# Emitting the very last load of a 90-degree rotation ahead of an output, and giving that output the freed load buffer

## The chip, the cores and the metric

The kernel runs on one core of one Trainium2 chip. The metric is the device time of one execution in microseconds (us). "Time" below is that figure; "landing", "issue" and all other moments are read from a profile of one execution and count from the start of its span. In the profile of the kernel before, the last landing stands at 1264.37, the span is 1265.4 and the time of that execution 1267.31, so a time is about 2.9 us above the last landing. "Landing" needs a word: a transfer is shared out among up to 16 DMA engines, and each of them leaves a record when its share has arrived. The last of these records is the landing of the transfer.

## The reference

```python
def setup_inputs():
    return {"x": np.random.randn(8192, 8192).astype(np.float32), "k": 1}

def reference(x, k):
    return np.rot90(x, k)
```

An 8192 x 8192 matrix of 4-byte values is read once (268 MB) and written once (268 MB), turned by 90 degrees.

## The kernel before

The matrix is cut into macro tiles of 1024 x 4096. For each, eight loads of 128 rows (2 MB each) go out on SP's queue. VectorE reverses each row block by 128-column blocks into small "ar" tiles, PE (the matrix engine) transposes these into PSUM, ScalarE copies PSUM into an output tile "ot" and issues its store, also 2 MB. The last macro tile is cut into two of half height, here called A and B. Each has four loads (LA0 to LA3, LB0 to LB3) and four stores (A0 to A3, B0 to B3). M0 to M7 are the stores of the last full macro tile.

```python
a_pool = ctx.enter_context(tc.tile_pool(name="a_pool", bufs=2))   # load buffers
r_pool = ctx.enter_context(tc.tile_pool(name="r_pool", bufs=63))  # reversed chunks
o_pool = ctx.enter_context(tc.tile_pool(name="o_pool", bufs=3))   # output buffers
...
def load(r0, rt, c0):            # a generator: one row block for each next()
    ...
    for t in range(rt):
        ...
        a = a_pool.tile([P, W], dt, tag="a")     # (early loads: o_pool)
        nc.sync.dma_start(out=a[:], in_=x[...])
        for j in range(W // CH):
            ar = r_pool.tile([P, CH // P, P], dt, tag="ar")
            nc.vector.tensor_copy(out=ar[:], in_=...)   # the reversal
            chunks[t, j] = ar
        yield chunks

def store(r0, rt, c0, chunks, end):   # a generator: one output for each next()
    ...
    for i, g0 in enumerate(range(0, W // P, G)):
        if end and i % 2:
            ot = a_pool.tile([P, F], dt, tag="a")
        else:
            ot = o_pool.tile([P, F], dt, tag="o")
        ...                                  # 32 transposes, 2 copies
        nc.scalar.dma_start(out=dst, in_=...)
        yield
...
*_, chunks = load(*before_last)                    # LA0 .. LA3
outputs = store(*before_last, chunks, True)
rows = load(*last)
for _ in range(last[1] - 1):
    next(rows)                                     # LB0 .. LB2
next(outputs)                                      # A0
chunks = next(rows)                                # LB3
for _ in outputs:                                  # A1 .. A3
    pass
for _ in store(*last, chunks, True):               # B0 .. B3
    pass
```

There is one reversed chunk more (64) than there are tiles for them (63). So LB3's last reversal needs a chunk that A0's transposes give back, and A0 has to stand ahead of that reversal in the program.

Of the kernel before, what the change touches and what calls it, by code (L numbers as in the profile page):

```python
# [2 lines left out]

# [5 lines left out]

P = 128  # L10




R = 1024
RT = R // P
LAST = [4, 4]
W = 4096
CH = 512
F = 4096  # L20
FP = 2048


def whole_reads(nc):






    for fn in nc.m.functions:
        for block in fn.blocks:
            for n, ins in enumerate(block.instructions):
                if not isinstance(ins, mybir.InstDMACopy):
                    continue
                src = ins.ins[0]
                ap = [list(d) for d in src.ap]
                if len(ap) == 3 and ap[2][0] == 1 and ap[1][0] == ap[2][1]:
                    ap = [ap[0], [1, 1], [1, ap[1][1] * ap[2][1]]]
                    block.instructions[n] = copy.replace(  # L40
                        ins,
                        ins=[copy.replace(src, ap=ap)],
                        ant_dge_precooked=False,
                    )


def macro_tiles(N, M):

    tiles = [(r0, RT, c0) for r0 in range(0, N, R) for c0 in range(0, M, W)]
    r0, _, c0 = tiles.pop()  # L50
    for n in LAST:
        tiles.append((r0, n, c0))
        r0 += n * P
    return tiles


@with_exitstack
def kernel(
    ctx: ExitStack,
    tc: tile.TileContext,  # L60
    x: bass.AP,
    k: bass.AP,
    out: bass.AP,
):
    nc = tc.nc
    assert k == 1, f"only k=1 supported, got {k}"
    nc.at_finalize(whole_reads)

    N, M = x.shape
    dt = x.dtype  # L70

    consts = ctx.enter_context(tc.tile_pool(name="consts", bufs=1))
    ident = consts.tile([P, P], dt)
    make_identity(nc, ident)

    a_pool = ctx.enter_context(tc.tile_pool(name="a_pool", bufs=2))
    r_pool = ctx.enter_context(tc.tile_pool(name="r_pool", bufs=63))
    o_pool = ctx.enter_context(tc.tile_pool(name="o_pool", bufs=3))
    psum_pool = ctx.enter_context(
        tc.tile_pool(name="psum", bufs=2, space=bass.MemoryType.PSUM)  # L80
    )

    loads = 0

    def load(r0, rt, c0):





        nonlocal loads
        chunks = {}
        for t in range(rt):


            if loads < RT and loads % 5 >= 2:
                a = o_pool.tile([P, W], dt, tag="o")
            else:
                a = a_pool.tile([P, W], dt, tag="a")
            loads += 1  # L100
            nc.sync.dma_start(  # L101
                out=a[:], in_=x[r0 + t * P : r0 + (t + 1) * P, c0 : c0 + W]
            )
            for j in range(W // CH):
                ar = r_pool.tile([P, CH // P, P], dt, tag="ar")
                nc.vector.tensor_copy(  # L106
                    out=ar[:],
                    in_=a[:, j * CH : (j + 1) * CH].rearrange(
                        "r (b m) -> r b m", m=P
                    )[:, :, ::-1],  # L110
                )
                chunks[t, j] = ar
            yield chunks

    def store(r0, rt, c0, chunks, end):





        rows = rt * P
        PW = 1
        while 2 * PW * rows <= FP:
            PW *= 2
        G = PW
        while 2 * G * rows <= F:
            G *= 2
        for i, g0 in enumerate(range(0, W // P, G)):
            if end and i % 2:
                ot = a_pool.tile([P, F], dt, tag="a")  # L130
            else:
                ot = o_pool.tile([P, F], dt, tag="o")
            o = ot[:, : G * rows].rearrange("m (g f) -> m g f", g=G)



            lead = r0 == 0 and c0 == 0 and i in (4, 6)
            S = PW if lead or (end and r0 + rows == N and g0 + G == W // P) else G


            ps = {}

            def transposes(t, ws):
                for w in ws:
                    g = g0 + w
                    nc.tensor.transpose(  # L146
                        ps[w // PW][:, PW - 1 - w % PW, t * P : (t + 1) * P],
                        chunks[t, g * P // CH][:, g % (CH // P), :],
                        ident,
                    )  # L150

            def psum_tile(h):
                pt = psum_pool.tile([P, FP], mybir.dt.float32, tag="ps")
                ps[h] = pt[:, : PW * rows].rearrange("m (g f) -> m g f", g=PW)

            if i == 0 and (rt == RT or r0 + rows < N):
                for h in range(G // PW):
                    psum_tile(h)
                for t in range(rt):
                    transposes(t, range(G))  # L160
            for h in range(0, G, PW):
                if h // PW not in ps:
                    psum_tile(h // PW)
                    for w in range(h, h + PW):
                        for t in range(rt):
                            transposes(t, [w])
                nc.scalar.copy(o[:, G - PW - h : G - h, :], ps[h // PW])  # L167

                done = h + PW
                if done % S == 0:  # L170
                    top = M - c0 - (g0 + done) * P
                    dst = out[top : top + S * P, r0 : r0 + rows].rearrange(
                        "(g m) f -> m g f", g=S
                    )
                    nc.scalar.dma_start(  # L175
                        out=dst, in_=o[:, G - done : G - done + S, :]
                    )
            yield

    tiles = macro_tiles(N, M)  # L180
    *most, before_last, last = tiles
    for m in most:
        *_, chunks = load(*m)
        for _ in store(*m, chunks, False):
            pass


    *_, chunks = load(*before_last)
    outputs = store(*before_last, chunks, True)
    rows = load(*last)  # L190
    for _ in range(last[1] - 1):
        next(rows)
    next(outputs)
    chunks = next(rows)
    for _ in outputs:
        pass
    for _ in store(*last, chunks, True):
        pass


# [1 line left out]
_INS = ['x', 'k']  # L202
_OUTS = [((8192, 8192), 'float32')]

_NUMBERS = {'k': 1}


# [26 lines left out]
```

## Time and profile before

| | before |
|---|---|
| time, median of 6 runs | 1267.64 us (1267.44 to 1268.09) |
| bytes moved | 537 MB at 428 GB/s in mid-run |
| busiest compute engine | PE, 57% |
| A0's copies start / A0 issued | 1214.80 / 1218.46 us |
| last landing | 1264.37 us |

The prediction shows the page's lines on traffic and chain, the timeline of the tail and the DMA share by stretches. Two more lines of the page are needed to read them, those of the DMA issues: what is moved, who issues it, how often, the KB of one, and the median us from issue to landing.

```profile
a<-in_x_dram SPq DMA_DIRECT2D x128, 2048.0 KB, 16.6
out_dram<-ot ACTq DMA_DIRECT2D x125, 2048.0 KB, 25.7
```

A store takes 25.7 us from its issue until it has landed, although 2 MB at 428 GB/s are 4.9 us of traffic. By this sum most of a store's life is spent in a queue behind other transfers.

### The profile page before, as it was taken

Reading aid. Unit: us, or ns where it says so; the run is one execution under the profiler, and the core shown is the slowest. Engines: PE = TensorE matmul, PEld = TensorE weight load, DVE = VectorE, ACT = ScalarE, POOL = GpSimd, SP = SyncE. Lnnn points to the kernel's source line nnn. Section 1 sums busy time; section 2 is a strip of 40 time slices with the busy share of each in tenths; the row PEclk is TensorE's granted clock in tenths of the full one; section 3 lists DMA queues with packets and bytes.
Section 4 is the critical chain, followed back from the end, with each engine's and each line's share of the span. In section 5 each row is a group of like instructions: output and inputs, shape, how many; then the busy total and the mean of one; then the engine's idle time right before and its main releaser. Section 6 shows DMA issues by size and latency. Waiting matters only on the chain.

```text
span 1265.4 us, 10391 instructions
## 1 busy us (share of the span) xinstructions
PE 721.2 (57%) x4096; PEld 680.0 (54%) x4096; DVE 355.2 (28%) x1024; ACT 466.6 (37%) x257; POOL 0.7 (0%) x6
## 2 busy tenths in 40 slices
PE   1554555566555565565655666556555566566573
PEld 1453555566545565555645655456555555555573
DVE  4423223322232222322233222322233222332210
ACT  0432433433334333343334333343333433343354
POOL 0000000000000000000000000000000000000000
PEclk9977777767777768777687776866867867767787
DMA  9999999999999999999999999999999999999998
GB/s 398 428 428 430 427 428 429 429 431 428 428 429 427 430 429 430 428 430 429 428 428 430 429 430 428 428 430 428 429 430 428 429 427 430 426 428 427 428 380 355
DMA packets 37345, 537.55 MB, mean 425 GB/s; under 512 B 4144, under 2 KB 4144, under 8 KB 4144
## 3 DMA queue, kind: packets, MB, share of 16 engines
q10 hardware_dynamic: 18864, 268.44, 50.0%
q1 hardware_dynamic: 18432, 268.44, 49.7%
q8 instruction: 32, 0.52, 0.2%
q14 instruction: 17, 0.14, 0.0%
HBM read 268.44 MB, written 268.44 MB: 424 GB/s over the span
## 4 chain that ended last, share of the span: by engine, by line
DMA 84%; ACT 13%; issue 1%; PE 0%; ACTq 0%; DVE 0%; SPq 0%
DMA out_dram<-ot 81%; ACT ot L167 13%; DMA a<-in_x_dram 3%; PE pt L146 0%; ACTq L175 0%; DVE ar L106 0%; ACTq L167 0%; SPq L101 0%
## 5 line engine op out<-in xcount | busy, mean ns | idle before, releaser
L146 PE MATMUL pt<-ident,ar 128*128 128x128 f32 x4096 | 721.2, 357 | 526.2 <-ACT ot L167 470.2
L146 PEld LDWEIGHTS pt<-ident,ar 128*128 128x128 f32 x4096 | 680.0, 191 | 567.2 <-ACT ot L167 505.0
L167 ACT COPY ot<-pt 128x2048 f32<-128x2048 f32 x256 | 465.3, 1870 | 757.5 <-DMA out_dram<-ot 719.6
L106 DVE COPY ar<-a 128x512 f32<-128x512 f32 x1024 | 355.2, 420 | 861.8 <-DMA a<-in_x_dram 705.7
L167 ACT ACT_TABLE_LOAD x1 | 1.3, 1283 | 25.6 <-DVE ar L106 25.6
masks.py:199 POOL TENSOR_SCALAR_AFFINE_SELECT ident<-ident 128x128 f32<-128x128 f32 x1 | 0.3, 292 | 0.1
masks.py:197 POOL MEMSET ident<- 128x128 f32 x1 | 0.2, 204 | 0.3 <-POOLq L215 0.3
L215 POOL MEMSET const-bfloat16-1.0<- 128x1 bf16 x1 | 0.1, 101 | 0.0
L215 POOL MEMSET const-uint8-127<- 128x1 uint8 x1 | 0.1, 101 | 0.0
L215 POOL MEMSET const-float32-0.0<- 128x1 f32 x1 | 0.1, 98 | 0.2 <-issue 0.2
L215 POOL MEMSET const-float32-1.0<- 128x1 f32 x1 | 0.1, 98 | 0.0
## 6 DMA issues: line engine op xcount, KB each, us to landing
a<-in_x_dram SPq DMA_DIRECT2D x128, 2048.0 KB, 16.6
out_dram<-ot ACTq DMA_DIRECT2D x125, 2048.0 KB, 25.7
out_dram<-ot ACTq DMA_DIRECT2D x6, 1024.0 KB, 26.8
```

What stands on the lines that cost most here:

```text
L106: nc.vector.tensor_copy(out=ar[:], in_=a[:, j * CH : (j + 1) * CH].rearrange("r (b m) -> r b m", m=P)[:, :, ::-1],)
L146: nc.tensor.transpose(ps[w // PW][:, PW - 1 - w % PW, t * P : (t + 1) * P], chunks[t, g * P // CH][:, g % (CH // P), :], ident,)
L167: nc.scalar.copy(o[:, G - PW - h : G - h, :], ps[h // PW])
L215: nc = _bacc.Bacc("TRN2", target_bir_lowering=False, num_devices=1)
```

## The change

The last load, LB3, is emitted ahead of A0 and only its reversal stays behind. With LB3 placed, the next load buffer to come free is LB2's, and A0 takes it in place of an output buffer whose earlier store is still in flight. The intent is to let A0 be copied and stored earlier.

```diff
             nc.sync.dma_start(
                 out=a[:], in_=x[r0 + t * P : r0 + (t + 1) * P, c0 : c0 + W]
             )
+            yield chunks
             for j in range(W // CH):
...
         for i, g0 in enumerate(range(0, W // P, G)):
-            if end and i % 2:
+            if end and i % 2 == 0:
                 ot = a_pool.tile([P, F], dt, tag="a")
...
     rows = load(*last)
-    for _ in range(last[1] - 1):
+    for _ in range(2 * last[1] - 1):
         next(rows)
     next(outputs)
     chunks = next(rows)
```

## The prediction

> **What bounds the kernel now.** I name the outputs at the end: M0 to M7 are the eight 2 MB stores of the last full macro tile, A0 to A3 those of the last macro tile but one (half height), B0 to B3 those of the last. LB0 to LB3 are the four loads of the last tile. The change touches nothing before A0, so I read the page for the whole, then only the last 60 us.
>
> The page first: its head, the slices of moved bytes, the DMA queues and the chain.
>
> ```profile
> span 1265.4 us, 10391 instructions
> ...
> GB/s 398 428 428 430 427 428 429 429 431 428 428 429 427 430 429 430 428 430 429 428 428 430 429 430 428 428 430 428 429 430 428 429 427 430 426 428 427 428 380 355
> ...
> HBM read 268.44 MB, written 268.44 MB: 424 GB/s over the span
> ...
> DMA out_dram<-ot 81%; ACT ot L167 13%; DMA a<-in_x_dram 3%; PE pt L146 0%; ACTq L175 0%; DVE ar L106 0%; ACTq L167 0%; SPq L101 0%
> ```
>
> The kernel moves 537 MB at a flat 428 GB/s and no compute engine passes 57%: it is bound by the DMA engines. Only the last two of the 40 slices (31.6 us each) fall short, by 48 and 73 of 428 GB/s: 3.5 us and 5.4 us of full traffic. Anything that a change of the tail can win lies within those 9 us, 0.7% of the time.
>
> Next the timeline of the tail. Columns: start, length, engine, line, operation, and in brackets the idle time before and what ended it.
>
> ```profile
> 1205.64 3.63 ACT L167 COPY ot<-pt 128x2048 f32<-128x2048 f32 x2 [6.19 <-DMA out_dram<-ot]
> 1207.55 1.57 PEld L146 LDWEIGHTS pt<-ident,ar 128*128 128x128 f32 x8 [3.87 <-ACT ot L167]
> 1207.56 6.42 PE L146 MATMUL pt<-ident,ar 128*128 128x128 f32 x32 [3.63 <-ACT ot L167]
> 1209.30 0.55 ACTq L175 DMA_DIRECT2D out_dram<-ot  x1
> ...
> 1214.22 2.77 DVE L106 COPY ar<-a 128x512 f32<-128x512 f32 x8 [7.99 <-DMA a<-in_x_dram]
> 1214.80 3.63 ACT L167 COPY ot<-pt 128x2048 f32<-128x2048 f32 x2 [5.53 <-DMA out_dram<-ot]
> 1216.72 5.01 PEld L146 LDWEIGHTS pt<-ident,ar 128*128 128x128 f32 x32 [2.98 <-ACT ot L167]
> ...
> 1218.46 0.55 ACTq L175 DMA_DIRECT2D out_dram<-ot  x1
> ```
>
> The stores at 1209.30 and 1218.46 are M7 and A0. A0's copies stood from 1209.27 to 1214.80 for the landing of M5 (issued 1189.68, landed 1214.72), whose buffer they take: this is the wait that the change aims at. But A0's transposes, the 32 matmuls from 1207.56, ran until 1213.98 by the modelled ends.
>
> Then the DMA engines around it, in the view by stretches. The last two columns are their mean busy share and GB/s.
>
> ```profile
> 1215.00:1218.00 3.00, 1.28 (x6) 1.28 (x7) 2.00 (x6) 3.00 (x2) 0.00 (x0) 0.75 0.59 251
> 1218.00:1219.00 1.00, 1.00 (x7) 1.00 (x6) 0.00 (x0) 0.43 (x1) 0.00 (x0) 0.50 0.24 98
> 1219.00:1220.00 1.00, 1.00 (x7) 1.00 (x6) 0.00 (x0) 0.00 (x0) 0.00 (x0) 0.54 0.70 295
> 1220.00:1240.00 20.00, 17.46 (x151) 16.12 (x150) 0.00 (x0) 17.03 (x10) 0.00 (x0) 1.00 0.97 406
> 1240.00:1259.50 19.50, 6.91 (x61) 6.36 (x59) 0.00 (x0) 8.43 (x5) 0.00 (x0) 0.77 1.01 418
> 1259.50:1260.50 1.00, 0.00 (x0) 0.00 (x0) 0.00 (x0) 0.00 (x0) 0.00 (x0) 0.50 0.60 246
> 1260.50:1264.50 4.00, 0.00 (x0) 0.00 (x0) 0.00 (x0) 0.00 (x0) 0.00 (x0) 0.50 0.14 57
> ```
>
> There is a hole before A0's store: 3 x 0.41 + 0.76 + 0.30 = 2.3 us of idle mean. It looks like the prize. But a mean over 16 engines can hide which of them are idle, and the last row is the warning: for the final 4 us the share is 0.14, about 2 of 16. So I took the trace's landing records, of which each DMA leaves 16. First, 14th and last of the 16, in us:
>
> ```
> store   issued    first    14th     last     last minus last of the store before
> M5     1189.68  1199.7   1208.3   1214.72
> M6     1199.48  1209.4   1214.4   1219.57   4.85
> M7     1209.30  1215.8   1219.3   1224.50   4.93
> A0     1218.46  1225.0   1225.8   1229.48   4.98
> A1     1223.93  1230.5   1232.0   1234.47   4.99
> B2     1245.50  1255.4   1257.5   1259.38
> B3, two halves               last 1261.87 and 1264.37: 2.49 and 2.50
> ```
>
> From M5 to the end the last landing comes every 4.85 to 5.00 us, also across the hole. Two landings of each store trail the other 14 by about 5 us there. One sixteenth of 2 MB is 8 packets of 16,384 bytes, and a packet in this stage takes 621 ns (median of the packet records from 1225 to 1250 us): 8 x 0.621 = 4.97 us. So the two trailing engines work without a pause, at their own rate; the hole belongs to the 14 leading ones. The end, 1264.37, is M7's last landing plus eight outputs: 1224.50 + 8 x 4.98 = 1264.3.
>
> **What the Trainium skill says.** "DMA: Bandwidth & Descriptors", section "Why a DMA increments its semaphore by 16 and not by 1": up to 16 engines finish independently, each posts its own increment, and only the full 16 means landed. The spread of up to 15 us within M5 agrees. The same page, "Queues, rings and completion order": each engine consumes a ring's descriptors in order. The regular spacing above fits that. The same page, "Specifications": about 27 GiB/s an engine. The trace has 16,384 bytes in 611 ns in mid-run, 26.8 GB/s, somewhat less; I use the trace.
>
> **The change part by part.**
>
> 1. The early load. The instruction order of both builds is the same on every engine, and LB3 is the last of the loads on SP's queue in both, waiting for the same reversal of LB1 (it was issued at 1196.5, long before A0). What the diff emits earlier, the machine already did in that place: 0.
>
> 2. The reversal behind. The order on VectorE is the same too, with the same waits: 0.
>
> 3. The buffers. This alone is real: eight copies on ScalarE have other waits in the build. A0 now takes LB2's buffer and waits for LB2's reversal, which ended at 1203.46 + 2.77 = 1206.23, in place of M5's landing at 1214.72. It is then held by its transposes: its first copy can start between 1213.3 (four of the last eight matmuls still to come, at 24 weight loads in 4.42 us, so 0.7 us before the end) and 1214.0. That is 0.8 to 1.5 us earlier; I take 1.2. A0's store goes out at about 1217.3.
>
> 4. The copies after it. A1 takes M5's buffer (1214.72), against a start at 1220.26 - 1.2 = 1219.1: free. A2 takes LB3's, reversed at 1214.22 + 2.77 = 1216.99, against 1223.4: free. A3 waits for M6 (1219.57) against 1227.7; B0 for A0 (1229.48) against 1232.0; B1 for M7; B2 for A2 (last landing 1239.45) against 1240.6; B3 for A1 (1234.47). All free; B2's margin, 1.2 us, is the least. So the eight stores go out about 1.2 us earlier each.
>
> 5. What that does to the end. For the leading 14 engines the hole shrinks by 1.2 us, and their last packets end at about 1259.2 and not 1260.4. The two trailing ones start A0 at 1224.50 in either kernel: A0 was issued 6.0 us before that already, and needed only to be there by then. They go on at 4.98 us an output: 1264.4. Gain: 0. With less idling beside them their M6 and M7 might lose the small advantage seen (4.85 and 4.93 against 4.98), at most 0.13 + 0.05 = 0.2 us; I take +0.05.
>
> Sum: 1267.57 + 0.05 = **1267.6 us**.
>
> **The rivals.** First, the whole pull-forward reaches the end, if the 16 engines share their backlog or the trailing two have a pause: 1267.57 - 1.2 = 1266.4. For it: the hole of 2.3 us, and the chain of waits, which goes from M5's landing through A0's copies into ScalarE. Against it: the even last landings; and the chain ends with the last copy, 14.6 us before the last landing, so it does not follow what ends the span. Second, a new wait takes the place: B2's copies wait for A2, should the pull be larger than 1.2 us. Even then each late store has 8 to 14 us from issue to landing, at most 5 of them its own transfer, so a delay of a microsecond is absorbed: again 1267.6. Third, the different moment of the instruction fetches (the page's q8, 16 KB each, one packet of about 0.6 us on one engine) hits a trailing engine in the tail: +0.6, so 1268.2.
>
> **Range and chances.** The three runs of before lie within 0.6 us. I add the first rival's -1.2 below and the third's +0.6 above, with a little for another run of the chip: 1266.4 to 1268.5. 2% is 25 us, and the tail holds 9: faster 0.005, same 0.99, slower 0.005.
>
> **What would show it.** Right: A0's copies wait for PE, not for a store; its store issues at 1217 to 1217.7; the hole is narrower; the last stretch with a share near 0.14 is longer, about 5 us; the last landings of M6 to B3 stand where they did, within 0.2 us. Wrong: the last landings move with the issue, by 1 us or more, or any load of the last tile is issued at another time.

## The result, and the profile after

| | runs | median | range |
|---|---|---|---|
| before | 6 | 1267.64 us | 1267.44 to 1268.09 |
| after | 6 | 1267.36 us | 1267.26 to 1267.99 |

The ratio is 0.9998, with a 95% interval of 0.9985 to 1.0011: the same. Ratios here are of fast runs of the same rounds, so they are not quite the ratio of the medians quoted.

The page of the changed kernel, in the same parts as before. The profiled execution took 1267.99 us, the slowest of the six.

```profile
span 1266.1 us, 10392 instructions
...
GB/s 399 426 428 430 428 429 427 430 429 429 429 429 429 430 428 427 430 429 430 428 430 428 429 429 428 430 428 428 430 430 428 429 429 428 428 428 428 427 399 328
...
DMA out_dram<-ot 79%; ACT ot L169 14%; DMA a<-in_x_dram 3%; PE pt L148 1%; ACTq L177 0%; DVE ar L108 0%; ACTq L169 0%; SPq L102 0%
```

The last but one slice rose from 380 to 399 GB/s and the last fell from 355 to 328. The traffic went forward by a slice, and the last slice, which holds the end, has less to do and is no shorter.

The timeline of the tail after the change; the columns are those of the prediction. The last two lines, B1's store and B2's copies, are read in the part on the prediction.

```profile
1206.29 3.63 ACT L169 COPY ot<-pt 128x2048 f32<-128x2048 f32 x2 [6.25 <-DMA out_dram<-ot]
...
1209.95 0.55 ACTq L177 DMA_DIRECT2D out_dram<-ot  x1
...
1209.98 4.01 PE L148 MATMUL pt<-ident,ar 128*128 128x128 f32 x24 [0.51 <-ACT ot L169]
1213.59 3.64 ACT L169 COPY ot<-pt 128x2048 f32<-128x2048 f32 x2 [3.66 <-PE pt L148]
1213.71 2.77 DVE L108 COPY ar<-a 128x512 f32<-128x512 f32 x8 [7.10 <-DMA a<-in_x_dram]
1215.50 3.50 PEld L148 LDWEIGHTS pt<-ident,ar 128*128 128x128 f32 x32 [1.76 <-ACT ot L169]
...
1217.25 0.55 ACTq L177 DMA_DIRECT2D out_dram<-ot  x1
...
1239.28 1.13 ACTq L177 DMA_DIRECT2D out_dram<-ot  x1
1240.51 3.63 ACT L169 COPY ot<-pt 128x2048 f32<-128x2048 f32 x2 [1.25 <-DMA out_dram<-ot]
```

A0's copies start at 1213.59, released by PE and no longer by a store, and A0 is issued at 1217.25, 1.2 us earlier than before, although M7 was issued 0.65 us later here (1209.95 against 1209.30). The pull-forward of A0 happened as foreseen. That of the stores behind it did not: A1 to B0 were issued 2.3 to 2.4 us earlier than before (A1 at 1221.56 against 1223.93), B2 1.3 us earlier (1244.17 against 1245.50), and the second half of B3 0.6 us later (1250.83 against 1250.19). A1 gained twice: its transposes began 1.2 us earlier, and their 32 weight loads took 3.50 us (at 1215.50) and not 5.01 (at 1216.72 before). PE's granted clock was 1.00 from 1215 to 1220 here, and 0.50 to 0.54 from 1217 to 1220 before. Whether the change or chance made that difference, no run was built to tell.

The DMA engines in the same stretches (the last two columns are the mean busy share of 16 engines and GB/s):

```profile
1215.00:1218.00 3.00, 2.49 (x23) 2.45 (x24) 1.49 (x5) 2.33 (x3) 0.00 (x0) 1.00 0.67 284
1218.00:1219.00 1.00, 1.00 (x12) 1.00 (x10) 0.00 (x0) 1.00 (x1) 0.00 (x0) 1.00 0.86 360
1219.00:1220.00 1.00, 0.42 (x5) 0.19 (x4) 0.00 (x0) 1.00 (x2) 0.00 (x0) 1.00 1.14 475
1220.00:1240.00 20.00, 17.22 (x150) 16.08 (x150) 0.00 (x0) 16.08 (x9) 0.00 (x0) 1.00 1.00 418
1240.00:1259.50 19.50, 5.01 (x44) 4.49 (x42) 0.00 (x0) 7.27 (x4) 0.00 (x0) 0.76 0.96 398
1259.50:1260.50 1.00, 0.00 (x0) 0.00 (x0) 0.00 (x0) 0.00 (x0) 0.00 (x0) 0.50 0.20 82
1260.50:1264.50 4.00, 0.00 (x0) 0.00 (x0) 0.00 (x0) 0.00 (x0) 0.00 (x0) 0.50 0.11 45
```

The hole shrank: its idle mean between 1215 and 1220 fell from 2.3 us to 3 x 0.33 + 0.14 = 1.1 us. It came back at the other end. In 1259.5 to 1260.5 the share fell from 0.60 to 0.20, and the four us after that still run at 0.11, about two engines of 16. Each DMA leaves 16 landing records, and they tell who is early and who late (us):

```
              before                        after
store   first    14th     last       first    14th     last
M5     1199.7  1208.3   1214.72     1199.5  1209.5   1214.91
M7     1215.8  1219.3   1224.50     1216.4  1220.0   1224.98
A0     1225.0  1225.8   1229.48     1223.8  1225.0   1230.02
B2     1255.4  1257.5   1259.38     1253.7  1255.8   1260.04
B3b      -       -      1264.37       -       -      1265.04
```

(B3b is the second half of B3.) The first engine lands A0 1.2 us earlier and B2 1.7 us earlier (1255.4 to 1253.7). The last landing did not come forward: it is 0.2 us later at M5, which the change does not touch, and 0.7 us later at the end, in a profile that is of the slowest of the six runs. From M5 to the end it took 1265.04 - 1214.91 = 50.13 us, against 49.65 before.

### The profile page after: what moved, and what is told of

The parts are those of the page before. It is cut to its first block, busy times and chain, and to the rows that moved or that the text cites. A ratio compares the mean times of both kernels' runs of the same rounds, so it can differ in the third digit from the quotient of the medians.

```text
span 1266.1 us, 10392 instructions
## 1 busy us (share of the span) xinstructions
PE 718.2 (57%) x4096; PEld 678.6 (54%) x4096; DVE 355.4 (28%) x1024; ACT 466.7 (37%) x257; POOL 0.7 (0%) x6
## 4 chain that ended last, share of the span: by engine, by line
DMA 82%; ACT 14%; PE 1%; issue 1%; ACTq 1%; DVE 0%; SPq 0%
DMA out_dram<-ot 79%; ACT ot L169 14%; DMA a<-in_x_dram 3%; PE pt L148 1%; ACTq L177 0%; DVE ar L108 0%; ACTq L169 0%; SPq L102 0%
```

## The experiments

The theory: the end is set by two DMA engines that trail the other 14 (by some 5 us when M7 lands) and always have stores queued, so that when A0 is issued does not matter, as long as they do not run dry. The main rival: the end follows A0's issue, and the gain was lost elsewhere, in a new wait or by chance.

### The early load alone (built, not run)

Only the second `yield` and the doubled count, with `i % 2` left as it was. The built program has the same instructions in the same order with the same waits on all five engines as the kernel before. It is the same program, so there was nothing to time. The early emission only serves to make A0 take LB2's buffer and not LB1's.

### The buffers alone

```diff
-            if end and i % 2:
+            if end and i % 2 == 0:
```

> Only the buffer part of the change: A0, A2, B0, B2 take load buffers, but the last load LB3 stays behind A0 in the program. A0 then takes LB1's buffer and LB3 has to take LB2's, free only after LB2's reversal. Theory (the two trailing DMA engines set the end, they have a backlog of stores and never pause): LB3 is issued at about 1206.3 instead of 1196.5 and lands some 3 to 4 us later (about 1217.5 instead of 1214), A0 is stored at about 1217.3 as in the changed kernel, and the end does not move: 1267.5, within 0.7 us of before. Rival (the end follows the last load and what hangs on it): 3 to 4 us slower, 1271.

Measured: 1268.74 us median of 4 (1267.48, 1267.91, 1269.57, 1269.59) against 1267.25 of 7 runs of before; ratio 1.0007 (0.9991 to 1.0024). The four runs fall into two groups, and the profiled one is a slow one. Its landing records show the last engine of a store trailing the next by up to 3.2 us within the first 105 us, and by 2.0 to 4.1 us from 161 us to the end, against at most 1.8 us in any transfer of the kernel before. That is a thousand microseconds ahead of the first instruction that the change touches. So I ran it again.

> The buffer part alone once more: of its four runs two took 1267.5 and 1267.9, two 1269.6. In the profiled one of 1269.6 one engine trailed the next by over 2 us from 105 us on, long before any instruction that the change touches. If that was chance, most of these runs are at 1267.2 to 1268 with a seldom one near 1269.6, as the kernel before had once (1268.7); if the late load costs time, the median is 1268.5 or more again.

Measured: 1267.49 us median of 5 (1267.15 to 1267.67, and one of 1269.59) against 1267.40; ratio 1.0004 (0.9991 to 1.0016). The timeline of this profile has the late load (first line), M7's store at 1207.76 and A0's at 1215.58, and LB3's reversal at 1220.66:

```profile
1206.30 0.33 SPq L101 DMA_DIRECT2D a<-in_x_dram  x1
1207.76 0.55 ACTq L175 DMA_DIRECT2D out_dram<-ot  x1
...
1215.58 0.55 ACTq L175 DMA_DIRECT2D out_dram<-ot  x1
...
1220.66 2.77 DVE L106 COPY ar<-a 128x512 f32<-128x512 f32 x8 [14.39 <-DMA a<-in_x_dram]
```

LB3 was issued 9.8 us later than before (1206.30 against 1196.5) and landed 6.4 us later (1220.57 against 1214.13; I had forecast 3 to 4). The last landing was 1264.19, against 1264.37 before. Neither the moment of the last load nor that of A0's store (2.9 us earlier than before) shows in the end. Three of nine runs were near 1269.6. Whether the late load makes that group more frequent was not settled. The 2 us themselves were in the one profiled run long before the load.

### Holding A0's store back: a dose and its response

In the changed kernel A0's first copy was made several times over, with the same values:

```diff
+                if end and i == 0 and h == 0 and r0 + rows < N:
+                    for _ in range(2):        # 4 and 6 in the other two
+                        nc.scalar.copy(o[:, G - PW - h : G - h, :], ps[h // PW])
                 nc.scalar.copy(o[:, G - PW - h : G - h, :], ps[h // PW])
```

> The changed kernel with A0's first copy made three times instead of once (same values), which holds A0's store and all that follows on ScalarE back by 2 x 1.87 = 3.74 us. Theory: the trailing engines finish M7 at 1224.1 and 1225.0 and the store needs about 1.6 us from issue to its first packets, so A0 may be issued up to about 1222.5 without harm; here it is issued at 1217.25 + 3.74 = 1221.0. End unchanged, 1267.4 within 0.7 us; the spread between first and last landing of the last store falls from 6.3 us to about 2.6. Rival (the end follows the moment of A0's issue): +3.7, 1271.1.

> The same with six extra copies, 11.22 us: A0 is issued at about 1228.5, its first packets come at about 1230.1, when the last trailing engine has been idle since 1225.0. Theory: the end moves by the difference, about 5 us (4 to 6), to about 1272.4, and all 16 engines land within about 1 us of each other. Rival (the end follows the issue): +11.2, 1278.6.

The scheduler set other copies between the repeated ones, so the delay that was reached is not the one that I had worked out; I read the first store's issue from each profile instead. A third dose was chosen after these two:

> A middle dose. The runs with two and six extra copies showed that the scheduler lets A1's first copy in between, so the moment of issue is to be read and not taken from the number of copies: it was 1219.11 with two (0.65 us later than before the change, end unmoved) and 1226.95 with six (8.5 us later, end 6.0 us later). In this build seven copies of about 1.78 us stand between 1211.8 and the first store, so it is issued at about 1224.3, 5.8 us later than before the change, and its packets come at about 1225.9. Theory: the last trailing engine runs dry at about 1224.2 to 1225.0, so the end moves by 1 to 1.7 us, to about 1268.7 (1268.0 to 1269.5). Rival (the end follows the issue): 5.8 us, 1273.1.

| kernel | first store of A issued | against before | median of before, same rounds | time, median | change |
|---|---|---|---|---|---|
| after | 1217.25 | -1.2 | 1267.64 | 1267.36 | -0.3 |
| two extra copies | 1219.11 | +0.65 | 1267.25 | 1267.29 | 0.0 |
| four | 1224.28 | +5.8 | 1267.38 | 1271.34 | +4.0 |
| six (A1 is issued first) | 1226.95 | +8.5 | 1267.25 | 1273.22 | +6.0 |

From -1.2 to +0.65 us the end stands still. Between +0.65 and +8.5 it does move, by less than the issue does: part of the delay is free. That is the theory's shape and not the rival's, which had +0.65, +5.8 and +8.5. With six copies the end moved by 6.0 us, at the edge of the forecast (4 to 6). In size the forecast for four copies was too low: 4.0 us and not 1.0 to 1.7. The stretches of its profile show why:

```profile
1220.00:1223.00 3.00, 2.38 (x11) 2.38 (x12) 0.00 (x0) 2.97 (x3) 0.00 (x0) 0.61 0.13 55
1223.00:1224.00 1.00, 1.00 (x7) 0.90 (x5) 0.00 (x0) 1.00 (x1) 0.00 (x0) 0.50 0.00 0
1224.00:1225.00 1.00, 0.95 (x8) 0.71 (x7) 0.00 (x0) 0.96 (x2) 0.00 (x0) 0.98 0.00 0
1225.00:1226.00 1.00, 1.00 (x12) 1.00 (x10) 0.00 (x0) 1.00 (x1) 0.00 (x0) 1.00 0.68 262
```

The share is 0.13 (two engines) until 1223 and then 0.00: here the trailing engines ran dry. M7's last landing is 1223.85 and A0's first is 1230.9, less 4.98 for its own transfer 1225.9: 2.05 us of pause. A0's last landing is 1232.60, so one engine is another 1.7 us behind the first (the 15th landing is at 1231.1). The pause and this add up to the 3.8 us by which the step from M7 to A0 (8.75 us) exceeds 4.98. An instruction-fetch packet of 16 KB lies at 1225.26 in that trace, and one at 1228.00 with six copies, where one engine lands 1.3 us behind the first. In the kernel before, too, one more engine falls back beside each of the two such packets of the tail: at 1225.30 the 14th landing goes from 0.6 us (A0) to 1.4 us (A1) behind the 13th, at 1244.52 the 13th from 0.03 us (A3) to 1.3 us (B0) behind the 12th. There those engines lead by more than that, and the end does not show it; with four and six copies all engines start level. That the packet ran on the very engine that was late is argued and not shown, as the packet records do not name the engine.

### Which engines trail

The last store (1 MB, 128 partitions) of the changed kernel was cut by partitions (the edit is shortened):

```diff
-  nc.scalar.dma_start(out=dst, in_=src)
+  for m in [98, 15, 7, 8]:        # second probe: [108, 6, 5, 4, 3, 2]
+      nc.scalar.dma_start(out=dst[m0 : m0 + m], in_=src[m0 : m0 + m]); m0 += m
```

> The changed kernel with the last store (1 MB, 128 partitions) cut into four of 98, 15, 7 and 8 partitions, to see from the landings which engines trail: by the Trainium skill they run on the lowest-numbered 14, 15, 7 and 8 engines. If the trailing two are always the same engines, the count of late landings in each piece tells where they sit: none in any piece but 15 would make one of them the 15th and one the 16th; one in the 8 and none in the 7 would make it the 8th. The time is about that of the changed kernel, within 2 us.

> As the first probe, in which both late landings were in every piece, also in that of 7 engines; so the two trailing engines are the same for every piece and among the first seven. Now the last store is cut into 108, 6, 5, 4, 3 and 2 partitions (12, 6, 5, 4, 3 and 2 engines by the same page): the first piece without a late landing tells below which number both sit. Two late in the piece of 12; in the smaller ones I have no forecast. Time within 3 us of the changed kernel.

The Trainium skill, "DMA: Bandwidth & Descriptors", section "Why a DMA increments its semaphore by 16 and not by 1", says that such a DMA runs on the lowest-numbered k engines, k being the largest divisor up to 16 of the partitions here, and that the remaining 16 - k are posted at once. The records agree in the counts: 14, 15, 7 and 8 landings in the first probe and 12, 6, 5, 4, 3 and 2 in the second, each with one earlier update. Which engines they are, the records do not name; that they are the lowest-numbered rests on the page. Both probes were correct; single runs of 1268.93 and 1269.16 us. The late landings:

```
piece on engines  12   6   5   4   3   2          (first probe: 14  15   7   8)
late landings      2   2   2   1   0   0                         2   2   2   2
of the second probe, landings in us:
5 engines: 1259.8 1260.1 1261.9 | 1265.7 1266.3
4 engines: 1260.8 1261.2 1262.2 | 1266.0
3 engines: 1261.6 1261.9 1262.5
```

A piece of three engines has no late landing, one of four has one, one of five has two. So, if the pieces use the lowest-numbered engines, the late ones are the same two in every piece, the fourth and the fifth.

### Load for the leading engines, and load for the trailing ones

Three short loads that nobody uses were put behind LB3 in the changed kernel. 51 rows go to three engines and 85 to five; the bytes for one engine are the same.

```diff
     chunks = next(rows)
+    for e in range(3):
+        spare = r_pool.tile([P, CH // P, P], dt, tag="ar")
+        nc.sync.dma_start(out=spare[:51]..., in_=x[:51, e * CH : (e + 1) * CH])   # or 85
```

> The changed kernel with three more loads of 51 rows of 2 KB behind LB3, into spent reversal tiles and never used. 51 rows go to 3 engines, 17 rows each, so the first three engines get 3 x 17 x 2 KB = 104 KB more, 3.9 us at 26.6 GB/s, and none of the others. The second probe put the two trailing engines at fourth and fifth place, and the first three lead by 4 to 6 us. Theory: the lead swallows it, end within 0.8 us of the changed kernel, 1267.4 (up to 1268.2). Rival (the end follows the total of bytes): 313 KB at 424 GB/s, 0.7 us; this run does not tell these two apart, the next does.

> The same with 85 rows, which go to 5 engines, 17 rows each: the first five engines get 104 KB more, now with the trailing fourth and fifth among them. Theory: they have no lead to swallow it, the end moves by the whole 3.9 us (3.3 to 4.6), to about 1271.3. Rival (total of bytes): 522 KB at 424 GB/s, 1.2 us, 1268.6.

Measured: with 51 rows 1267.07 us (ratio 1.0000, 0.9988 to 1.0013), with 85 rows 1271.26 us (ratio 1.0030, 1.0016 to 1.0044), against 1267.40 of before: -0.3 and +3.9, where 3.9 was forecast. The stretches at the end, 51 rows first:

```profile
1260.50:1264.50 4.00, 0.00 (x0) 0.00 (x0) 0.00 (x0) 0.00 (x0) 0.00 (x0) 0.50 0.09 37
```

```profile
1260.50:1264.50 4.00, 0.00 (x0) 0.00 (x0) 0.00 (x0) 0.00 (x0) 0.00 (x0) 0.50 0.12 51
1264.50:1269.00 4.50, 0.00 (x0) 0.00 (x0) 0.00 (x0) 0.00 (x0) 0.00 (x0) 0.50 0.08 35
```

With 85 rows the share of two engines goes on beyond 1264.5, where the other kernel is done. The last landings there are 1268.0 and 1268.1 us, and the 14th is 1260.2: exactly two engines. The extra loads themselves show which: three landings of the first come at 1214.9 to 1215.6 and two at 1224.9 and 1225.6, so of the five engines that carry it three lead and two trail. This is the sharpest of the tests: the same bytes for one engine cost nothing on the first three, and their whole transfer time once the fourth and fifth get them too.

### Where the early store should show

If leading engines set the end, the earlier A0 has to pay. A1's store was cut so that the first three engines get three times their share, in both kernels:

```diff
-  nc.scalar.dma_start(out=dst, in_=...)
+  for m in ([51, 77] if end and r0 + rows < N and i == 1 else [P]):
+      nc.scalar.dma_start(out=dst[m0 : m0 + m], in_=o[m0 : m0 + m, ...]); m0 += m
```

> The kernel before, with A1's store cut into 51 and 77 partitions, which go to the first 3 and the first 11 engines. The first three engines so get 17 + 7 = 24 partitions of 16 KB instead of 8, 16 packets more, 10 us at 0.622 us each. That uses up their lead of 4 to 6 us, and the end is theirs: their first packets of A0 come when A0 is issued, so A0 lands there at 1225.0 as it did on all leading engines, then 8 x 4.98 + 9.96 us follow: last landing 1274.8, time 1277.7 (the time is 2.9 us above the last landing in the profile of before). Within 1.5 us. Rival (total of bytes, which is unchanged): 1267.4.

> The changed kernel with the same cut of A1. Theory: where engines that stood idle in the hole set the end, the earlier A0 must show: A0 lands there at 1223.8 instead of 1225.0, so the end is 1.2 us earlier than that of the kernel before with the same cut (0.8 to 1.6), about 1276.5. Rival (the earlier store is worth nothing anywhere, for instance since the DMA engines are limited as a whole): the same time, within 0.3 us.

> The kernel before with the cut of A1, once more. In the profiles of both cut kernels the last landing came 59.3 us after A0's issue, and in both all of the tail was 1 to 3 us later than usual from before the change's first instruction. With the usual issues, 1218.46 before and 1217.25 after, that makes 1218.46 + 59.3 + 2.9 = 1280.7 here and 1279.4 for the changed kernel (three of its four runs: 1279.2 to 1279.9). So if the 2.7 us between the two was partly chance, this median is 1280.0 to 1281.3; if it is 1282 or more again, the early A0 is worth more here than its own 1.2 us, and why stays open.

| | runs (us) | median |
|---|---|---|
| before, A1 cut | 1281.67, 1282.37, 1282.38, 1285.12 | 1282.38 |
| before, A1 cut, again | 1281.90, 1282.07, 1282.23, 1282.58 | 1282.15 |
| after, A1 cut | 1279.18, 1279.46, 1279.91, 1282.59 | 1279.69 |

By the medians the changed kernel is now the faster one, by 2.5 to 2.7 us. Ratios to the uncut kernel before are 1.0121 (1.0105 to 1.0136) and 1.0117 (1.0100 to 1.0133), against 1.0094 (1.0077 to 1.0111): 0.2% between the two cut kernels, with intervals that overlap at their ends, though the runs do not, save for the 1282.59. The direction is as foretold, and the rival's equal times are not what was seen; a trace of it is missing, as the profile kept of the changed kernel is of its slow run (1282.59), and that kernel was not run again.

The size is not as foretold. 1.2 us was forecast between the two, and both totals were 3 to 5 us too low. The sum behind the totals also counts eight outputs after A0 where seven follow (A1 to A3 and B0 to B3); put right, the forecasts are 1272.7 and 1271.5, and the misses 8 to 10 us. The records of the repeat show where they are: the 24 packets of A1 kept the slowest of the first three engines busy from 1224.6 to 1249.4, 24.8 us and not 24 x 0.622 = 14.9. ScalarE was held for 5.38 us by the two issues of A1 as well (0.55 us for one otherwise). The repeat (1282.15) speaks against chance in the kernel before. But in the first profiles of both cut kernels the same 24 packets took 22.8 us, so 2 us of the difference can lie in them and not in A0's issue. Why the packets took longer, and how much of the 2.5 to 2.7 us is the pull, stays open.

## Why the prediction was right

The time foretold was 1267.6 (1266.4 to 1268.5), the measured one 1267.36. The number alone decides little, as the first rival's 1266.4 lies at the edge of the same range; the timeline and the experiments decide.

1. **The early load and the reversal behind, 0 each.** Right, and exactly so: the early load alone builds the same program as before. (The whole change has one wait instruction more on PE, 10392 instructions against 10391; the order is otherwise the same.) In the changed kernel LB3 was issued at 1196.8, against 1196.5.
2. **A0's copies are held by PE and start 0.8 to 1.5 us earlier.** Right: 1213.59, released by PE, 1.2 us earlier; the store at 1217.25, foretold 1217.3.
3. **The later copies find their buffers free, with 1.2 us the least margin at B2, and eight stores go out 1.2 us earlier each.** Right on the buffers, wrong on the stores: A1 to B0 came 2.3 to 2.4 us earlier and the last half of B3 0.6 us later: A1's transposes were faster, as said under the timeline, and the issues from B0 on took longer. B2's margin shrank to 0.3 us (the last two lines of that timeline). The view puts the wait down to A2's landing, the latest event, at 1240.12 (0.67 us later than before). But ScalarE was busy issuing B1's store until 1240.41, so the buffer was free by then. The pause is longer than the 0.67 us before because that issue took 1.13 us and not 0.55. So the second rival's wait did not occur here.
4. **The trailing two engines set the end and gain nothing.** Right for the profiled tail, and shown from three sides: the end does not move for issues from 1.2 us earlier to 0.65 us later, it does move once these engines run dry, and an extra load of 3.9 us for each engine counts on them alone.
5. **+0.05 us for the trailing engines, since the others idle less beside them.** The sign may be right and the size is too small in the profiles: M5 to the end took 49.65 us before, 50.13 after, and 50.15 with two extra copies, about 0.5 us more. The medians (-0.3 us) do not show it, so it is not a finding. The sign that the prediction named, last landings from M6 to B3 within 0.2 us of before, was missed for this reason: they came 0.36 us (M6) to 0.74 us (A3) later, of which 0.19 was there at M5. Its sign of being wrong, landings that move with the issue by 1 us or more, did not appear.
6. **The first rival (1266.4)** is out by the same tests. **The third**, an instruction fetch on a trailing engine, was not seen in the changed kernel, but a cost of its kind, 1.3 to 1.7 us on one engine, was with four and six extra copies. I had left it out of the forecast for those. Its size was too small as well: a fetch packet takes 0.93 to 1.03 us in the kernel before, and not 0.6.
7. **"8 to 14 us from issue to landing"** for the late stores was misread: from A0 on the records have 10.5 to 14.2. The argument, that a microsecond of delay is absorbed, stands.

What this does not settle: why just the fourth and fifth engine trail. Their distance to the 14th landing grows over the whole run (the 15th landing comes at most 0.24 us after the 14th in the stores issued from 104 to 161 us, and 6.1 us in the median in those from 988 to 1200 us, in the kernel before), so it is gathered slowly and not made in the tail. The runs point to taking work off these two as the way to a faster kernel; none did it. In the probes only the pieces of three and two engines avoid them. By an estimate from the lead of those three, about 4 us each: if stores worth y us of engine time in all are taken off the even spread and given to these three, each of them gets y/3 - y/16 more, which may be 4 us, so y is 4 / 0.27 = 15; each trailing engine loses y/16, so the gain is 0.9 us, too little to be told from the scatter. A build that sent the last store by GpSimd, to reach other engines, did not compile. So no kernel here is faster than the one before.

## What to carry to other kernels

Before you shorten a wait ahead of a transfer, look at how long its queue is: where stores take 10 to 26 us from issue to landing for 5 us of their own, as here, an earlier issue may only make the queue longer. A mean DMA share with a hole in it is not yet idle time to be won; look at the landings of each transfer one by one, because here the engines with no hole set the end. And a scheduler may already issue a load where you want it, so compare the built instruction orders before you expect anything from moving a line.

## What the Trainium skill lacked or had wrong

- "DMA: Bandwidth & Descriptors", section "Latency and other measured facts", says that engines 7 and 15 are usually slower than the others, with a best guess at the cause that concerns DMAs issued from GpSimd only. Here all transfers are issued from SP and ScalarE, and by the probes the fourth and the fifth of the 16 trailed, by 4 to 6 us behind the first engine at the end of a run of 1265 us, in stores that go evenly to all 16. That such a lag builds up in the course of a run with even transfers (0.24 us early, 6.1 us late) is on no page that I read.
- "Runtime: NRT & Kernel Launch", section "Instruction fetch mechanics", calls the cost of crossing a 16 KiB boundary mostly hidden, for the engine that executes; what the fetch costs the transfers beside it is not said. The trace of the kernel before has 32 such packets of 16 KB, at 0.93 to 1.03 us each. Beside one of 1.56 us a DMA engine landed 1.7 us late and the end came later (four extra copies); that this packet was the cause is argued only.
- No page that I read gives the time that an issue takes on ScalarE when several stores are queued: 0.55 us otherwise, 1.0 to 1.1 us for three of the last stores after the change, 2.1 and 2.5 us for the two halves of the last store before it, 5.4 us for two with A1 cut.
